# Linear ReLU attention: four engine programs jump to a fresh instruction block at the start, and wait for the last store at the end

## The chip, the core and the metric

The kernel runs on one core of a Trainium2 chip. A core has five engines, each with a program of its own: TensorE (PE in the tables; its weight loads are PEld), VectorE (DVE), ScalarE (ACT), GpSimd (POOL) and SyncE (SP). They meet through semaphores. Data moves between the large memory (HBM) and the on-chip memory (SBUF) by DMA, issued here by SP, ACT and POOL and carried out by 16 DMA engines. The metric is the device time of one launch in microseconds (us), lower is better.

## The reference

Q, K and V have shape (8, 12, 512, 64), that is 96 heads of 512 rows, in 32-bit floats. Each head is independent:

```python
Q_feat = np.maximum(0, Q)
K_feat = np.maximum(0, K)
KV = np.einsum('bhkd,bhkv->bhdv', K_feat, V)
K_sum = np.sum(K_feat, axis=2)
numerator = np.einsum('bhqd,bhdv->bhqv', Q_feat, KV)
denominator = np.einsum('bhqd,bhd->bhq', Q_feat, K_sum)
return numerator / (denominator[:, :, :, None] + 1e-10)
```

## The kernel before, in words

The work is cut into NO = 12 blocks of 8 heads. A block of Q, of K or of V is 1 MB in HBM, 128 partitions of 8 KB each, and a block of the output is 1 MB as well, so 48 such transfers are all the traffic. Most loads turn the numbers into bf16 on their way, so 512 KB arrive in SBUF.

The program of each engine is written out by hand in the order of the source; no scheduler moves anything.

- SP issues the load of K of block 0 (line 94), and at the end the stores of the last two blocks (`store`, line 117, called from line 134). Then it waits for the semaphores of all 12 stores (line 318) and clears the semaphores (line 321).
- ACT issues the load of V of block 0 (line 95). Its first compute instruction waits for ID to be 4 (line 207), which says that the masks are there. For each block it then moves results from PSUM to SBUF.
- POOL issues Q of block 0 (line 96), makes the identity matrix (lines 119 and 121), and then issues the loads of blocks 1 to 11 in the order K, V, Q (`load`, line 109). The ring of input buffers holds RING = 6 blocks, so from block 7 on a load waits until its buffer has been read. In between it issues the stores of blocks 0 to 9 (line 117), each as soon as `norm` has written that block.
- DVE clears buffers and builds masks (lines 276 to 295), adds the last step to ID, and then for each block prepares K and V (`prep`, lines 237 and 241), copies Q (`stage`, line 247), and divides (`denominators`, lines 265 to 273, and `norm`, line 259).
- PE waits for ID to be 4, then runs a loop of 12 turns (line 189). A turn (`turn`) transposes Q (line 158), multiplies K with V (line 167), transposes the previous block's results back (`back`, line 148), and computes the denominators (line 176) and numerators (line 184) of its own. After the loop, `back(0)` and `back(1)` do the transposes of the last block. The loop's head is put at the start of a 256-instruction block of PE's program by the loop's `head_slot` argument; the builder emits an alignment and a jump for that.

The output buffer ring has NOUT = 9 blocks, so `norm` of blocks 9, 10 and 11 waits until the store of the block nine before has ended. Each store has a semaphore of its own, `stored[o]`, and every DMA adds 16 to its semaphore, one for each DMA engine that has finished its part.

The times further down rest on how instructions get to an engine: the trace shows DMA packets of kind "instruction" on two queues of their own, q8 and q14.

Of the kernel before, what the change touches and what calls it, by code (L numbers as in the profile page):

```python
# [5 lines left out]
def kernel(  # L6
# [18 lines left out]
    NO = B * H // 8  # L25
    assert NO * 8 == B * H and R == 16
    RING = 6
    NOUT = 9
    RUNS = (1,) * 11
    HEAD = 4  # L30

# [4 lines left out]
    PE, PL, VE, AC, SP = nc.tensor, nc.gpsimd, nc.vector, nc.scalar, nc.sync  # L36
# [6 lines left out]
    def sb(name, shape, dt):  # L43
        return nc.alloc_sbuf_tensor(name, shape, dt)[:]
# [3 lines left out]
    def sems(*names):  # L48
        new = [nc.alloc_semaphore(n) for n in names]
        handles.extend(new)  # L50
        return new
# [8 lines left out]
    q_all = sb("q_all", [P, RING + 1, U * P], bf16)  # L60
    o_sb = [sb(f"o_sb{i}", [P, RQ, D], fp32) for i in range(NOUT)]
    k8, v8 = o_sb[0], o_sb[1]
# [18 lines left out]
    ID, STG, PR0, PR1, DEN, NRM0, NRM1, DV = sems(  # L81
        "id", "stg", "pr0", "pr1", "den", "nrm0", "nrm1", "dv")
# [1 line left out]
    CQ0, CQ1, CK0, CK1, CB0, CB1, CD, CO0, CO1 = sems(  # L84
        "cq0", "cq1", "ck0", "ck1", "cb0", "cb1", "cd", "co0", "co1")
    landed = {}
    stored = sems(*[f"st{o}" for o in range(NO)])

    def land(name):
        landed[name], = sems(name)  # L90
        return landed[name]


    SP.dma_start(out=k8.rearrange("p r d -> p (r d)"), in_=Kr[0]).then_inc(land("k0"), 16)
    AC.dma_start(out=v8.rearrange("p r d -> p (r d)"), in_=Vr[0]).then_inc(land("v0"), 16)
    PL.dma_start(out=q_all[:, RING], in_=Qr[0], single_packet=True).then_inc(land("q0"), 16)  # L96
    run_of = {0: 0}

# [15 lines left out]
    def store(eng, o):  # L114
        eng.wait_ge(NRM1, o + 2)
        kw = {"single_packet": True} if eng is PL else {}
        eng.dma_start(out=Or[o], in_=o_sb[(o + 2) % NOUT].rearrange("p r d -> p (r d)"), **kw).then_inc(stored[o], 16)  # L117

# [4 lines left out]
    o, done = 1, 0  # L123
    for n in RUNS:
        while done < o + n - 1 - RING - HEAD + 1:
# [4 lines left out]
    assert o == NO  # L130
    for i in range(done, NO - 2):
        store(PL, i)
    for i in range(NO - 2, NO):
        store(SP, i)

# [10 lines left out]
    def back(j):  # L146
        for v in range(8):
            t = PE.transpose(ps_o[j][:, P * v:P * v + P], ot[:, 8 * j + v].rearrange("p h c -> p (h c)"), ident32)  # L148
        t.then_inc((CB0, CB1)[j], 1)
# [35 lines left out]
                              start=True, stop=True, skip_group_check=True)  # L185
            t.then_inc((CO0, CO1)[j], 1)

    PE.wait_ge(ID, 4)
    with nc.Fori(1, NO + 1, engines=bass.OrderedEngineSet([PE.engine]), head_slot={PE.engine: 0}) as i:
        turn(i)  # L190
    PE.wait_ge(OT, NO + 1)
    back(0)
    back(1)


    def v_rows(o, g):
# [7 lines left out]
    def v_scalar(o):  # L204
        arrived(AC, "v", o)
        if o == 0:
            AC.wait_ge(ID, 4)
        AC.activation(vo[0][:, :, 1, 2:D + 2], v_rows(o, 0), Act.Copy, scale=mask_v[:, 1:2]).then_inc(VC, 1)  # L208

    v_scalar(0)  # L210
    for o in range(NO):
        for j in range(2):
            AC.wait_ge((CQ0, CQ1)[j], o + 1)
            AC.activation(qt_sb[:, j * (U // 2):(j + 1) * (U // 2)],  # L214
                          ps_q[j].bitcast(bf16).rearrange("p (u f) -> p u f", u=U // 2), Act.Relu)
        AC.wait_ge(CK1, o + 1)
        for s in range(2):
            for c in range(2):
                t = AC.copy(  # L219
                    kvd[64 * c:64 * c + 64, s::2, c * D1:c * D1 + D1].rearrange("p (g t) d -> p g t d", t=2),  # L220
                    ps_kv[64 * s:64 * s + 64, :, 0:2 * (D + 2)].rearrange(
                        "p g (t d) -> p g t d", t=2)[:, :, :, c:c + D1])
        t.then_inc(KVD, 1)
        if o + 1 < NO:
            v_scalar(o + 1)
        for j in range(2):
            AC.wait_ge((CO0, CO1)[j], o + 1)
            t = AC.copy(ot[:, :, 4 * j:4 * j + 4],  # L228
                        ps_o[j].rearrange("p (h u c) -> p u h c", h=4, u=U))
        t.then_inc(OT, 1)  # L230


    def prep(o, g):

        arrived(VE, "k", o)
        for s in range(2):
            VE.tensor_scalar(kf[g][:, :, s, :], k_rows(o, g), scalar1=0.0,  # L237
                             scalar2=mask_k[:, s:s + 1], op0=Alu.max, op1=Alu.mult)
        arrived(VE, "v", o)
        for t in range(1 + g):  # L240
            x = VE.tensor_scalar(vo[g][:, :, t, 2:D + 2], v_rows(o, g), scalar1=mask_v[:, t:t + 1],  # L241
                                 scalar2=None, op0=Alu.mult)
        x.then_inc((PR0, PR1)[g], 1)
# [5 lines left out]
    def norm(o):  # L249
        dst = o_sb[(o + 2) % NOUT]  # L250
        if o >= NOUT:
            VE.wait_ge(stored[o - NOUT], 16)
        VE.wait_ge(DV, 2 * o + 2 + DV0)
        if o == NOUT - 1:
            VE.wait_ge(VC, 1)
        for j in range(2):
            rs = slice(R * j, R * j + R)
            VE.wait_ge((CB0, CB1)[j], o + 2)
            VE.tensor_tensor(dst[:, rs], ps_o[j].rearrange("p (r d) -> p r d", d=D),  # L259
                             rec[o % 2][:, rs].unsqueeze(2).to_broadcast([P, R, D]),  # L260
                             op=Alu.mult).then_inc((NRM0, NRM1)[j], 1)
# [42 lines left out]
    for o in range(NO):  # L304
# [7 lines left out]
        if o + 1 < NO:  # L312
            prep(o + 1, 1)
    norm(NO - 1)


    for s in stored:
        SP.wait_ge(s, 16)
    used = sorted(s.num for s in handles)
    assert used == list(range(used[0], used[-1] + 1))  # L320
    SP.sem_clear(range(used[0], used[-1] + 1))
# [28 lines left out]
```

## Time and profile before

| | |
|---|---|
| median of three runs | 124.9 us (124.57 to 125.02) |
| the profiled execution's own time | 124.66 us |
| its span, first to last instruction | 123.4 us |
| busy: DVE, PE, ACT, POOL | 89.3, 87.4, 79.4, 27.5 us |
| HBM read and written | 37.75 and 12.58 MB |
| loads issued by POOL, issue to landing | 33.1 to 36.7 us |
| the last two stores, issued by SP, issue to landing | 8.4 us |

The page has a row for each engine with its busy share in 40 slices of the span, one for the DMA engines in the same slices, a table of the DMA queues, the chain of work that ended last, and the costliest groups of instructions. A group's row gives its line, engine and operation, the tiles, the count, the busy time, the mean duration, and how long the engine stood idle just before it and for what. A table by stage gives for each stretch of the span the busy time of PE, PEld, DVE, ACT and POOL with the number of instructions, the granted TensorE clock, the share of the DMA engines in use and the GB/s that they moved.

### The profile page before, as it was taken

To read this page: it belongs to the slowest core of one execution; us is meant where nothing else is said; L and a number is where in the kernel's file an instruction comes from. 1 tells how busy PE (TensorE), PEld (TensorE's weight loads), DVE (VectorE), ACT (ScalarE), POOL (GpSimd) and SP (SyncE) were. 2 spreads that over 40 slices of the span, in tenths; PEclk is the share of its full clock that TensorE was granted. 3 is DMA by queue.
4 is the path that set the end of the run, shared out by engine and by line. 5 is a ranking of instruction groups with operands and counts; after the bars stand their busy time and mean duration, and the time that the engine had idled before them with its cause. 6 is when DMAs were issued, how large, how long until landed. Compare 5 with 4: busy or idle time off the path is not lost.

```text
span 123.4 us, 3380 instructions
## 1 busy us (share of the span) xinstructions
PE 87.4 (71%) x1456; PEld 75.9 (62%) x1456; DVE 89.3 (72%) x178; ACT 79.4 (64%) x109; POOL 27.5 (22%) x50
## 2 busy tenths in 40 slices
PE   0000099998998979799897998979449939977400
PEld 0000099986886868688686877958429928947200
DVE  3737906599989899998989989897395497091600
ACT  0043063999988888898888889888539649542000
POOL 3999500050240804309101001010010001000000
PEclk9999999999999999999999999999985995996775
DMA  3999999999999999999999999999999999999994
GB/s 43 369 344 217 213 213 213 213 215 213 214 213 213 213 215 213 214 214 217 214 213 214 213 214 221 371 217 214 375 222 214 343 425 428 425 422 433 420 425 170
DMA packets 6918, 32.57 MB, mean 264 GB/s; under 512 B 768, under 2 KB 768, under 8 KB 5120
## 3 DMA queue, kind: packets, MB, share of 16 engines
q0 software_dynamic: 6336, 28.31, 92.2%
q1 hardware_dynamic: 432, 3.15, 6.6%
q10 hardware_dynamic: 144, 1.05, 2.2%
q8 instruction: 2, 0.03, 0.1%
q14 instruction: 4, 0.03, 0.1%
HBM read 37.75 MB, written 12.58 MB: 408 GB/s over the span
## 4 chain that ended last, share of the span: by engine, by line
DMA 34%; issue 27%; POOL 18%; PE 8%; DVE 5%; ACT 1%; POOLq 0%; DVEq 0%
DMA q_all<-in_Q_dram 34%; POOL k_all L109 6%; POOL q_all L109 5%; POOL v_all L109 5%; DVE o_sb L259 5%; PE ps_o L148 4%; PE ps_kv L167 2%; PE ps_q L158 1%; PE ps_o L184 1%; POOL out_dram L117 1%; ACT ot L228 1%; POOL q_all L96 1%; POOL ident L121 0%; POOL ident L119 0%; POOLq L107 0%
## 5 line engine op out<-in xcount | busy, mean ns | idle before, releaser
L259 DVE TENSOR_TENSOR o_sb<-ps_o,rec 128x1024 f32<-128x1024 f32 x24 | 28.3, 1219 | 7.0 <-PE ps_o L148 6.7
L228 ACT COPY ot<-ps_o 128x1024 f32<-128x1024 f32 x24 | 24.2, 1013 | 10.3 <-PE ps_o L184 9.2
L167 PE MATMUL ps_kv<-vo,kf 64*128 64x132 bf16 x768 | 28.6, 230 | 0.7
L148 PE MATMUL ps_o<-ident,ot 128*128 128x128 f32 x208 | 27.1, 286 | 1.1 <-ACT ot L228 1.1
L167 PEld LDWEIGHTS ps_kv<-vo,kf 64*128 64x128 bf16 x768 | 24.8, 100 | 3.8 <-DVE vo L241 2.3
L214 ACT ACTIVATE qt_sb<-ps_q 128x1024 bf16<-128x1024 bf16 x24 | 23.4, 1030 | 5.1 <-PE ps_q L158 5.1
L158 PE MATMUL ps_q<-ident,q_sb 128*128 128x128 bf16 x192 | 15.3, 243 | 15.4 <-DVE q_sb L247 15.4
L148 PEld LDWEIGHTS ps_o<-ident,ot 128*128 128x128 f32 x208 | 23.8, 146 | 2.7 <-ACT ot L228 1.4
L158 PEld LDWEIGHTS ps_q<-ident,q_sb 128*128 128x128 bf16 x192 | 13.2, 110 | 16.7 <-DVE q_sb L247 15.4
L219 ACT CAST kvd<-ps_kv 64x260 bf16<-64x260 f32 x48 | 18.0, 375 | 7.8 <-PE ps_kv L167 7.4
L184 PE MATMUL ps_o<-qt_sb,kvd 128*128 128x256 bf16 x96 | 15.0, 282 | 10.8 <-DVE o_sb L259 9.8
L237 DVE TENSOR_SCALAR kf<-k_all,mask_k 128x1024 bf16<-128x1024 bf16 x44 | 18.3, 459 | 5.6 <-PE ps_kv L167 5.4
L184 PEld LDWEIGHTS ps_o<-qt_sb,kvd 128*128 128x128 bf16 x96 | 7.7, 100 | 15.6 <-DVE o_sb L259 15.0
L241 DVE TENSOR_SCALAR vo<-v_all,mask_v 128x1024 bf16<-128x1024 bf16 x33 | 15.0, 483 | 0.9 <-DMA v_all<-in_V_dram 0.9
L109 POOL DMA_DIRECT2D k_all<-in_K_dram x11 | 8.4, 763 | 32.1 <-DVE vo L241 32.0
L117 POOL DMA_DIRECT2D out_dram<-o_sb x10 | 5.3, 533 | 40.7 <-DVE o_sb L259 40.7
L208 ACT ACTIVATE vo<-v_all,mask_v 128x1024 bf16<-128x1024 bf16 x11 | 12.7, 1155 | 0.3
L247 DVE COPY q_sb<-q_all 128x2048 bf16<-128x2048 bf16 x12 | 8.3, 694 | 5.7 <-DMA q_all<-in_Q_dram 5.7
L109 POOL DMA_DIRECT2D q_all<-in_Q_dram x11 | 8.9, 811 | 0.0
L109 POOL DMA_DIRECT2D v_all<-in_V_dram x11 | 7.6, 687 | 0.0
L176 PE MATMUL ps_q<-kvd,qt_sb 128*128 128x16 bf16 x192 | 6.9, 180 | 0.0
L176 PEld LDWEIGHTS ps_q<-kvd,qt_sb 128*128 128x128 bf16 x192 | 6.7, 96 | 0.2
(24 smaller groups left out, 27.8 us busy)
## 6 DMA issues: line engine op xcount, KB each, us to landing
out_dram<-o_sb POOLq DMA_DIRECT2D x10, 1024.0 KB, 39.8
q_all<-in_Q_dram POOLq DMA_DIRECT2D x12, 512.0 KB, 36.7
k_all<-in_K_dram POOLq DMA_DIRECT2D x11, 512.0 KB, 33.1
v_all<-in_V_dram POOLq DMA_DIRECT2D x11, 512.0 KB, 34.8
out_dram<-o_sb SPq DMA_DIRECT2D x2, 1024.0 KB, 8.4
o_sb<-in_K_dram SPq DMA_DIRECT2D x1, 1024.0 KB, 8.5
o_sb<-in_V_dram ACTq DMA_DIRECT2D x1, 1024.0 KB, 8.8
```

The source lines that it names most:

```text
L109: PL.dma_start(out=t[:, to:to + n], in_=X[o:o + n].rearrange("n p f -> p n f"), single_packet=True).then_inc(land(f"{c}{o}"), 16)
L148: t = PE.transpose(ps_o[j][:, P * v:P * v + P], ot[:, 8 * j + v].rearrange("p h c -> p (h c)"), ident32)
L158: t = PE.transpose(dst[:, u], q_sb[:, j * (U // 2) + u], ident)
L167: t = PE.matmul(ps_kv[:, half, 0:2 * (D + 2)].rearrange("p (t d) -> p t d", t=2), kf[g][rows, r].rearrange("p s d -> p (s d)"), vo[g][rows ...
L176: t = PE.matmul(ps_den[:, u], qt_sb[:, u], kvd[:, :, 0:2 * D1:2 * D1 - 1], start=True, stop=True, skip_group_check=True)
L184: t = PE.matmul(ps[:, h], kvd[:, 4 * j + h, 1:2 * D + 1], q[:, :, 4 * j + h, :], start=True, stop=True, skip_group_check=True)
L214: AC.activation(qt_sb[:, j * (U // 2):(j + 1) * (U // 2)], ps_q[j].bitcast(bf16).rearrange("p (u f) -> p u f", u=U // 2), Act.Relu)
L219: t = AC.copy(kvd[64 * c:64 * c + 64, s::2, c * D1:c * D1 + D1].rearrange("p (g t) d -> p g t d", t=2), ps_kv[64 * s:64 * s + 64, :, 0:2 * ...
L228: t = AC.copy(ot[:, :, 4 * j:4 * j + 4], ps_o[j].rearrange("p (h u c) -> p u h c", h=4, u=U))
L237: VE.tensor_scalar(kf[g][:, :, s, :], k_rows(o, g), scalar1=0.0, scalar2=mask_k[:, s:s + 1], op0=Alu.max, op1=Alu.mult)
L241: x = VE.tensor_scalar(vo[g][:, :, t, 2:D + 2], v_rows(o, g), scalar1=mask_v[:, t:t + 1], scalar2=None, op0=Alu.mult)
L259: VE.tensor_tensor(dst[:, rs], ps_o[j].rearrange("p (r d) -> p r d", d=D), rec[o % 2][:, rs].unsqueeze(2).to_broadcast([P, R, D]), op=Alu. ...
```

## The change

There are four edits. They compute nothing and move no data.

1. `at_line(eng)` emits an alignment: the next instruction of that engine's program stands at a multiple of FETCH = 128 instructions, and the engine gets there by a jump (no fill of empty instructions is allowed, `max_nops=0`). It is put into POOL's, ACT's and DVE's programs. On ACT it stands behind the issue of V of block 0; on POOL ahead of the issue of Q of block 0; on DVE ahead of its first instruction. SP gets none.
2. PE no longer waits for ID ahead of its loop, so that it jumps to the loop's block at once, and waits for its first tile there.
3. The stores' semaphores are merged: the stores of blocks 0, 1 and 2, which `norm` waits for, keep their own; those of blocks 3 to 9 share ALL, those of blocks 10 and 11 share LAST.
4. `hold(eng)` is put at the end of POOL's, PE's, ACT's and DVE's programs: it waits until ALL and LAST are complete, and then adds 1 to FIN. SP waits for FIN to be 4 in place of its twelve semaphores. On POOL the hold comes after its last store, on PE after `back(1)`.

```diff
+    FETCH = 128
...
-    stored = sems(*[f"st{o}" for o in range(NO)])
+
+    ALL, LAST, FIN = sems("all", "last", "fin")
+    stored = [sems(f"st{o}")[0] if o + NOUT < NO else ALL if o < NO - 2 else LAST for o in range(NO)]
...
+    def at_line(eng):
+
+        eng.addr_align(FETCH, offset=0, max_nops=0)
+
+    def hold(eng):
+
+        eng.wait_ge(ALL, 16 * (NOUT - 2))
+        eng.wait_ge(LAST, 32)
+        eng.sem_inc(FIN, 1)
+
...
     AC.dma_start(out=v8.rearrange("p r d -> p (r d)"), in_=Vr[0]).then_inc(land("v0"), 16)
+    for eng in (PL, AC, VE):
+        at_line(eng)
     PL.dma_start(out=q_all[:, RING], in_=Qr[0], single_packet=True).then_inc(land("q0"), 16)
...
         store(PL, i)
+    hold(PL)
     for i in range(NO - 2, NO):
         store(SP, i)
...
-    PE.wait_ge(ID, 4)
     with nc.Fori(1, NO + 1, engines=bass.OrderedEngineSet([PE.engine]), head_slot={PE.engine: 0}) as i:
         turn(i)
     PE.wait_ge(OT, NO + 1)
     back(0)
     back(1)
+    hold(PE)
...
         t.then_inc(OT, 1)
+
+    hold(AC)
...
     norm(NO - 1)
-
-
-    for s in stored:
-        SP.wait_ge(s, 16)
+    hold(VE)
+
+
+    SP.wait_ge(FIN, 4)
```

## The prediction

> **What bounds the kernel now.** I read the page's slices first, then its queues, then stages of the span, then single DMA windows, and last the trace's record of every DMA packet (queue, start, duration, size).
>
> ```profile
> span 123.4 us, 3380 instructions
> DMA  3999999999999999999999999999999999999994
> q8 instruction: 2, 0.03, 0.1%
> q14 instruction: 4, 0.03, 0.1%
> HBM read 37.75 MB, written 12.58 MB: 408 GB/s over the span
> ```
>
> The DMA row is full from the second slice to the last but one while no compute engine is above 72% busy. The packet records say the same: from 2.75 us on all 16 DMA engines work without a gap, an 8 KB packet every 0.307 us each. So the end is the start of the DMA stream, plus each engine's own packets, plus whatever else is put on that engine. Two small queues are something else: six packets of instructions, 16 KB on q8, 8 KB on q14. Windows of the DMA view place them:
>
> ```profile
> q8 instruction: 1, 0.02, 2.9%
> ...
> q14 instruction: 1, 0.01, 1.3%
> ...
> q14 instruction: 1, 0.01, 1.0%
> ...
> q8 instruction: 1, 0.02, 3.0%
> ```
>
> These come from the windows 11 to 13, 32 to 33.5 (97 to 98.5 and 105 to 106.5 show the same row), 49 to 51 and 114 to 116 us. By the packet records: q8 at 11.495 us (935 ns) and 114.339 (965 ns); q14 at 32.745 and 49.661 (322 ns), 97.455 and 105.547 (309 ns).
>
> Whose are they? DVE has begun 58 instructions by 29.0 us and 186 by 93.7, exactly 128 apart, and its two fetches would then lie 3.75 us later each, at 32.745 and 97.455. The same 3.75 us before the others: 7.74 us, when PE's jump into its loop (started 7.347, 309 ns) ends; 45.9, ACT's 46th instruction; 101.8, POOL's last; 110.59, PE just after its loop.
>
> ```profile
> L189 PEldq COMPARE_BRANCH  x13: 76/208/309, 7.3 to 110.3; - x13
> 2.70:121.20 118.50, 87.39 (x1456) 75.89 (x1456) 88.47 (x175) 79.39 (x109) 26.54 (x45) 0.95 1.04 273
> 121.20:121.60 0.40, 0.00 (x0) 0.00 (x0) 0.00 (x0) 0.00 (x0) 0.00 (x0) 0.50 0.31 123
> 121.60:122.20 0.60, 0.00 (x0) 0.00 (x0) 0.00 (x0) 0.00 (x0) 0.00 (x0) 0.50 0.23 96
> 122.40:122.70 0.30, 0.00 (x0) 0.00 (x0) 0.00 (x0) 0.00 (x0) 0.00 (x0) 0.50 0.07 27
> ```
>
> The first row is the loop's branch; the last leaves the loop at 110.279 + 0.076 = 110.355. Then stages of the span: the DMA share (last but one column) falls from full to 0.31, 0.23, 0.07. 0.23 of 16 is 3.7 engines: four are still working when twelve have ended. Laying each engine's packets end to end, twelve end at 121.20 to 121.59 us (middle 121.35), four at 122.22, 122.34, 122.69 and 122.715. The late ones are those that carried the fetches of 105.5 (POOL), 97.5 (DVE), 11.5 (PE) and 114.3 us (PE). A fetch costs its engine its packet and a longer packet behind it: among reads 0.3 to 0.4 us for 8 KB (322 and 0.04), 1.1 for 16 KB; among stores 0.3 (+0.35 at 97.5, +0.09 at 105.5) and for 16 KB 0.965 + 0.355 = 1.3. The lag is never made up. The last store's last landing is at 123.129 us, SP's final wait passes, and the clear ends the span:
>
> ```profile
> L318 SPq EVENT_SEMAPHORE  x6: 17/28/28, 117.0 to 123.1; - x6
> L321 SPq EVENT_SEMAPHORE_RANGE_CLEAR  x1: 145/145/145, 123.2 to 123.2; - x1
> ```
>
> The profiled execution took 124.66 us, 1.30 outside its span; the median of the three runs, 124.9, is 0.24 above it.
>
> **The change part by part.**
>
> **Jumps on POOL, ACT, DVE.** Each is one jump into a new block. The nearest row is PE's own: branch and next instruction 7.347 to 7.782, 0.44 us. Bounds: 0.2 (a taken branch inside the loop, 208 ns) and a full fetch of 3.75 us if the target is not there. I take 0.44, the same kind of jump. Six 8 KB fetches stand before the span (10.4 to 7.6 us before it), so targets should be there.
> - POOL: its jump stands ahead of the first Q load (issued 1.93 us, first packets 6.31), the identity memset, and all 33 loads behind. K and V of block 0, issued by SP and ACT at 1.40 before any jump, keep the DMA engines busy alone until about 8.1 (2.41 + 1.1 for the first packet, 15 more at 0.307). Slack 8.1 - 6.31 = 1.8 us against 0.44: nothing.
> - DVE: memsets and masks end at 7.2, K of block 0 lands at 9.94; the row "DVE kf L237 <- DMA o_sb<-in_K_dram" waits 2.8. Nothing. ACT waits for the masks (7.3), then a 1.28 us table load, and V lands at 10.15: 7.74 + 1.28 = 9.0. Nothing.
>
> **PE's wait for the masks removed.** PE enters its loop near 1.7 instead of 7.7 us and waits there for its first tile (ready 15.4, so the wait is only moved). Nothing on PE's work.
>
> **Fetches moved.** POOL's goes from 105.5, ACT's from 49.7, DVE's first from 32.7, PE's first from 11.5, to 1.7 us plus 1.0 (SP's K issue at 1.40 to its packets at 2.41, idle engines) to 3.75: start 2.7 to 5.5 us. That is mostly behind the first data, so each still costs its engine: 0.3 for 8 KB, 0.6 (two packets' time) to 1.1 for PE's 16 KB. DVE's remaining program, 210 - 6 = 204 instructions, fits no single block of 128; it crosses once at about its 134th instruction (64 to 66 us), a fetch near 69 among reads, 0.35. Engine ends from these: POOL's and ACT's 121.35 + 0.3 = 121.65, DVE's two 121.7, PE's first 122.0 to 122.7.
>
> **PE's second fetch stays.** PE's loop is 240 weight loads and matmuls, a move, a semaphore wait, an add and a branch: 244 of the 256 that 16 KB hold. Behind it come 32 more (`back(0)`, `back(1)`), so 12 instructions after leaving the loop PE steps into the next block, and 110.355 plus 12 issues of some 20 ns is 110.6, the 110.59 from above. The new `hold(PE)` comes after those 32. Neither the jump nor the hold moves this crossing, and the fetch at 114.3 still costs 1.3 on an engine that carries no other: 122.715, as before. That is why I count the other gains at nothing: this engine was already the last by 0.02 us.
>
> **The end.** SP's six waits (all but the last two long met) become one on FIN. After the last landing each of four engines passes a wait and adds to FIN, then SP clears. Before, landing to clear was 123.129 to 123.211, 0.08. New: an engine's wait (17 to 51 ns in the opening barrier's records), a hand-over (0.04, POOL's release at 0.621 to SP's next at 0.663), about 0.13: +0.05. Nothing is queued behind the holds; POOL's last store is ahead of its hold. What the engines do after the program now starts together instead of having been waiting: bounds 0 and 1.3 (all time outside the span once more); nearest, one opening barrier, 0.33. SP itself leaves last, as before, so I take 0 and keep 0.33 for the range.
>
> **Sum.** DMA start 0, last engine 122.715 - 0.0, end +0.05: 124.66 + 0.05 = 124.71 for such an execution, 0.24 more for the median: **124.95 us**.
>
> The Trainium skill, "Runtime: NRT & Kernel Launch", section "Instruction fetch mechanics", calls the price of crossing a block "one DMA tail-bump, mostly hidden", with blocks of 16 KiB. The trace shows 8 KB for all but PE, and the crossing hidden for the engine, but not for the DMA engine that carries it (0.3 to 1.3 us); by the page nothing could be won at all, which here gives the same sum.
>
> **The rivals.**
>
> *Faster: the last PE fetch goes too.* If it were caused by what follows PE's program, and not by the 12th instruction after the loop, the hold would put it behind the end. For: POOL's fetch came just at its end too. Against: the 3.75 us fit the crossing to 0.05 us; DVE's and ACT's ends brought none. Then the last engine is the one with PE's early fetch, 122.0 to 122.7: gain 0 to 0.7; if that packet comes before 2.4 us and is hidden, 121.7 and a gain of 1.0. I give 124.9 + 0.05 - 0.8 = 124.15, up to 123.9.
>
> *Slower: a jump's target has to be fetched.* Then POOL stands still 1.0 + 0.3 us (idle engines) to 3.75. The decisive point is 1.8 us: beyond it the DMA engines run dry between block 0's K and V and the first Q. 3.75 + 0.3 - 1.8 = 2.2 at worst, 127.1; 126.0 in the middle. Against: the six fetches before the span and PE's 0.44 us jump.
>
> The same page says, in the same section, that a taken branch to a target outside the two-page window stalls for a DMA fetch. No row here shows such a stall, and PE's jump to its next block did not.
>
> *Slower: the ends.* Holding four engines back lengthens what follows the last instruction by more than 0.6 us: 125.6 to 126.2. The 1.30 us outside the span allow it; the 0.33 us barrier speaks against it.
>
> *Fetches meet on one DMA engine.* Here all six lay on different ones. A PE and an 8 KB fetch on one: +0.3, 125.25.
>
> **How the numbers follow.** 0.5% (0.62 us) is about what a measurement can tell from no change. No change by the above, collisions included: 0.57. Faster rival 0.2, jump stall 0.13, ends 0.10. The first alone spans 124.4 to 125.4 (the 0.33 and 0.3 above, the scatter of runs of 0.2 below). To leave out no more than 2 in 10 the range reaches half into the rivals: 124.1 to 125.8.
>
> **What would show it.** Right: q8 still shows one packet near 114; q14 none after about 70 us; the share in the stage after the twelve engines end falls to one or two engines (0.06 to 0.12) instead of 0.23, yet the clear still starts at about 123.25; jumps on POOL, ACT, DVE of 0.2 to 0.5 us; first Q packets near 6.7. Wrong: no q8 packet after 100 us and an end before 122.6; POOL's first load after 4 us and a gap in the DMA row near 8 to 10; or a time outside the span well over 1.3 us.

## The result and the profile after

The changed kernel takes 125.35 us (median of 17 runs, 124.84 to 126.42), the kernel before 124.82 us (17 runs): a ratio of 1.0054, 95% interval 1.0034 to 1.0074. It is slower, clear of the noise; whether by more than the half per cent that I had set as the bound of "no change" the interval leaves open. 124.95 us was forecast, and the time lies inside the range of 124.1 to 125.8.

Each run lists its time and its span, so the time outside the span is their difference. Its median is 1.74 us after the change (17 runs, 1.67 to 1.82) and 1.33 us before (the 35 runs of the kernel before that were made with the first experiments, 1.26 to 1.46): +0.41. The median span is 123.6 against 123.5 us: +0.1, small beside the scatter of the spans before, 123.0 to 124.4. Together that is nearly the 0.53 between the medians. The profiled execution is one of the slower ones, 125.88 us: 1.79 outside a span of 124.09.

The page of the changed kernel, first lines, DMA row and instruction queues:

```profile
span 124.1 us, 3381 instructions
DMA  2999999999999999999999999999999999999994
q14 instruction: 4, 0.03, 0.1%
q8 instruction: 2, 0.03, 0.1%
```

There are still six instruction packets, but elsewhere. The DMA view of the windows 2 to 3, 4 to 7 (two rows), 68 to 70 and 114 to 116 us:

```profile
q14 instruction: 1, 0.01, 10.6%
...
q8 instruction: 1, 0.02, 2.2%
q14 instruction: 2, 0.02, 1.4%
...
q14 instruction: 1, 0.01, 1.0%
...
q8 instruction: 1, 0.02, 3.0%
```

The packet records give 2.43, 4.52, 5.12 (PE's), 6.30, 69.03 and 114.89 us (PE's second). Now the start on POOL, first after the change, then before:

```profile
5.05 0.67 POOL L111 DMA_DIRECT2D q_all<-in_Q_dram  x1 [4.60 <-issue]
5.72 0.22 POOL L134 MEMSET ident<- 128x128 bf16 x1
```

```profile
1.93 0.67 POOL L96 DMA_DIRECT2D q_all<-in_Q_dram  x1 [1.48 <-POOLq L16]
```

The first Q load issues 3.1 us later, and its first packets come at 7.97 us, 1.7 later than the 6.31 of before. What that does to the DMA engines is in the stages (DMA share and GB/s are the last two columns), after and then before:

```profile
2.70:7.50 4.80, 0.00 (x0) 0.00 (x0) 3.53 (x19) 0.00 (x0) 2.04 (x5) 1.00 0.89 357
7.50:9.25 1.75, 0.00 (x0) 0.00 (x0) 0.28 (x2) 1.28 (x1) 1.75 (x4) 1.00 0.96 260
...
121.20:121.60 0.40, 0.00 (x0) 0.00 (x0) 0.00 (x0) 0.00 (x0) 0.00 (x0) 0.50 0.97 410
121.60:122.20 0.60, 0.00 (x0) 0.00 (x0) 0.00 (x0) 0.00 (x0) 0.00 (x0) 0.50 0.72 300
122.40:122.70 0.30, 0.00 (x0) 0.00 (x0) 0.00 (x0) 0.00 (x0) 0.00 (x0) 0.50 0.26 109
122.70:123.40 0.70, 0.00 (x0) 0.00 (x0) 0.00 (x0) 0.00 (x0) 0.00 (x0) 0.50 0.09 35
```

```profile
2.70:7.50 4.80, 0.00 (x0) 0.00 (x0) 3.61 (x19) 0.20 (x1) 4.40 (x10) 1.00 0.89 332
7.50:9.25 1.75, 0.00 (x0) 0.00 (x0) 0.00 (x0) 1.08 (x1) 1.75 (x5) 1.00 1.01 346
```

From 7.5 to 9.25 us the rate falls from 346 to 260 GB/s: on several DMA engines K and V of block 0 run out before Q comes. Part of the fall is the type alone: a Q packet is listed with the 4 KB that it writes as bf16 and takes 0.32 us, a packet of K with 8 KB and 0.31. But the share drops too, by the packet records to 12 of 16 engines at work near 8.5 us, and some of the first Q packets are listed with 1.36 and 1.40 us instead of 0.32; I take it that they wait for their first data. By 11 us 347 data packets have ended, 388 before, and 41 packets of 0.32 us on 16 engines are 0.8 us. The median landing of the first Q block moves from 11.07 to 11.94 us, that of the 28th transfer from 72.61 to 73.38, the last landing from 123.13 to 123.89. So in this execution the whole stream is 0.8 us late, and at 121.6 to 122.2, where 0.23 of the DMA engines were at work before, 0.72 are. The profiled execution is one of the 4 of 17 whose span is 124.1 or longer; in the median the spans differ by the 0.1 from above.

The end, the four holds and SP's clear:

```profile
L104 ACTq EVENT_SEMAPHORE  x1: 1823/1823/1823, 122.1 to 122.1; - x1
L104 POOLq EVENT_SEMAPHORE  x1: 1823/1823/1823, 122.1 to 122.1; - x1
L104 DVEq EVENT_SEMAPHORE  x1: 1825/1825/1825, 122.1 to 122.1; - x1
L104 PEldq EVENT_SEMAPHORE  x1: 1823/1823/1823, 122.1 to 122.1; - x1
...
L339 SPq EVENT_SEMAPHORE_RANGE_CLEAR  x1: 135/135/135, 124.0 to 124.0; - x1
```

The rows are each hold's second wait, the one for LAST: it begins when ALL is full, at 122.1, and takes 1.82 us. From the last landing (123.891) to the clear (123.954) it is 0.063 us, before it was 0.082: inside the span the new ending costs nothing. What it costs comes behind the last instruction.

### The profile page after: what moved, and what is told of

Read it like the earlier page. It is cut to its first block, busy times and chain, and to the rows that moved or that the text cites. A ratio compares the mean times of both kernels' runs of the same rounds, so it can differ in the third digit from the quotient of the medians.

```text
span 124.1 us, 3381 instructions
## 1 busy us (share of the span) xinstructions
PE 86.6 (70%) x1456; PEld 75.1 (60%) x1456; DVE 89.0 (72%) x178; ACT 79.4 (64%) x109; POOL 27.9 (23%) x50
## 4 chain that ended last, share of the span: by engine, by line
DMA 34%; issue 28%; POOL 18%; PE 8%; DVE 5%; ACT 1%; POOLq 0%; DVEq 0%
DMA q_all<-in_Q_dram 34%; POOL k_all L124 6%; POOL q_all L124 6%; POOL v_all L124 5%; DVE o_sb L277 5%; PE ps_o L164 4%; PE ps_kv L183 2%; PE ps_q L174 1%; PE ps_o L200 1%; POOL out_dram L132 1%; ACT ot L244 1%; POOL q_all L111 1%; POOL ident L136 0%; POOL ident L134 0%; POOLq L122 0%
## 5 line engine op out<-in xcount | busy, mean ns | idle before, releaser
L183 PE MATMUL ps_kv<-vo,kf 64*128 64x132 bf16 x768 | 27.4, 224 | 0.7
L183 PEld LDWEIGHTS ps_kv<-vo,kf 64*128 64x128 bf16 x768 | 23.6, 97 | 3.9 <-DVE vo L259 2.3
L200 PE MATMUL ps_o<-qt_sb,kvd 128*128 128x256 bf16 x96 | 15.5, 289 | 11.3 <-DVE o_sb L277 10.7
L124 POOL DMA_DIRECT2D k_all<-in_K_dram x11 | 7.3, 661 | 29.5 <-DVE vo L259 29.3
L124 POOL DMA_DIRECT2D q_all<-in_Q_dram x11 | 8.3, 758 | 0.0
```

What stands on the lines that cost most here:

```text
L124: PL.dma_start(out=t[:, to:to + n], in_=X[o:o + n].rearrange("n p f -> p n f"), single_packet=True).then_inc(land(f"{c}{o}"), 16)
L183: t = PE.matmul(ps_kv[:, half, 0:2 * (D + 2)].rearrange("p (t d) -> p t d", t=2), kf[g][rows, r].rearrange("p s d -> p (s d)"), vo[g][rows ...
L200: t = PE.matmul(ps[:, h], kvd[:, 4 * j + h, 1:2 * D + 1], q[:, :, 4 * j + h, :], start=True, stop=True, skip_group_check=True)
```

## The experiments

**Which half of the change costs?** Two theories. E: the holds cost, outside the span, because what each engine does behind its program now begins only after the last store. J: the jumps cost, in the span and behind it, because the ends of the programs lie elsewhere in their blocks. First each half alone.

Holds without jumps (this diff and the next are against the changed kernel):

```diff
-    for eng in (PL, AC, VE):
-        at_line(eng)
...
+    PE.wait_ge(ID, 4)
     with nc.Fori(1, NO + 1, ...
```

> The kernel before with edits 3 and 4 alone: merged store semaphores, holds on four engines, FIN; no jumps, and PE waits for the masks again. Theory E (the holds cost, because what each engine does behind the program now starts together): time outside the span 1.75 us as after the change (1.30 before), span 123.3 to 123.5 as before, so 125.25 to 125.3 against 124.8. Theory J (the jumps cost, in the span and behind it, because the engines' ends lie elsewhere in their blocks): outside 1.30, time 124.8 as before.

Measured: 125.12 us (12 runs) against 124.9 (35 runs, shared by the first four kernels). Time outside the span 1.75 in the median, span 123.35 against 123.5. E names the outside right, to the hundredth; the span came out 0.15 shorter than it was before, so the total is 0.15 below what E expected, and the ratio of 1.0015 (0.9993 to 1.0036) alone would not tell it from no change. What tells it is the time outside the span, 1.65 to 1.83 in 12 runs against 1.26 to 1.46 before.

Jumps without holds, and the stores' semaphores as before:

```diff
-    def hold(eng):
...
-    hold(PL)
...
-    SP.wait_ge(FIN, 4)
+    for s in stored:
+        SP.wait_ge(s, 16)
```

> The kernel before with edits 1 and 2 alone: jumps on POOL, ACT and DVE, PE enters its loop at once; twelve store semaphores and SP's waits as before, no holds. Theory E: outside 1.30, span 123.1 to 124.6 as after, middle 123.55, time 124.85. Theory J: outside 1.75, time 125.3. Both: POOL's first load issues near 5.05 us, not 1.93.

Measured: 125.02 us, outside 1.31, spans 123.3 to 124.6 with a median of 123.65; POOL's first load at 5.148. E holds, J's second half falls: the jumps change nothing behind the program. What they may cost is in the span: 0.15 us in the median, which the ratio of 1.0017 (0.9991 to 1.0044) does not tell from nothing, and 3 of 12 spans of 124.1 or longer, against 3 of 35 before.

**Which engine's hold?** The hold-only kernel again, with the hold on one engine at a time; for PE, for instance (against the hold-only kernel):

```diff
-    hold(PL)
...
-    hold(AC)
...
-    hold(VE)
...
-    SP.wait_ge(FIN, 4)
+    SP.wait_ge(FIN, 1)
```

> The hold-only kernel with the hold on POOL alone; SP waits for FIN to be 1. If one engine's way out of the program is the slow one, one of the four single holds shows the time outside the span of 1.75 us and the others 1.30 to 1.35. If it is that all come at once, each of the four shows less than 1.75, between 1.30 and 1.6.

> The same with the hold on PE alone: outside 1.75 if PE's way out is the slow one, 1.30 to 1.35 if not; in between if it is that all come at once.

> The same with the hold on ACT alone: outside 1.75 if ACT's way out is the slow one, 1.30 to 1.35 if not; in between if it is that all come at once.

> The same with the hold on DVE alone: outside 1.75 if DVE's way out is the slow one, 1.30 to 1.35 if not; in between if it is that all come at once.

One execution each, its time and its span to the nanosecond (the second row, the kernel before run beside the four, has its span to 0.1 us only):

| held besides SP | time, us | span, us | outside, us |
|---|---|---|---|
| none (before) | 124.66 | 123.356 | 1.30 |
| none (before, beside the four) | 124.59 | 123.2 | 1.39 |
| ACT | 124.95 | 123.619 | 1.33 |
| DVE | 125.21 | 123.808 | 1.40 |
| PE | 125.20 | 123.670 | 1.53 |
| POOL | 125.15 | 123.450 | 1.70 |
| all four (hold only) | 125.16 | 123.475 | 1.69 |

It is one engine's way out, POOL's: held alone it costs as much as all four. ACT and DVE lie inside the scatter of the kernel before, 1.26 to 1.46, so nothing is shown of them. PE's 1.53 lies just above it; 12 runs each of two kernels further down that hold PE alone give 1.45 and 1.48 in the median, 0.12 to 0.15 above the 1.33 of before. I had expected all but one to be at 1.30 to 1.35. The merged semaphores cost nothing to be seen: ACT's kernel has them too. All four held cost no more than POOL: the ways out add up to no more than the slowest. My reading, which no trace shows because they end with SP's clear, is that they run beside each other, and that before the change all of them but SP's ran while the last stores were still moving.

**What does POOL's stall cost?** The changed kernel without POOL's jump:

```diff
-    for eng in (PL, AC, VE):
+    for eng in (AC, VE):
```

> The changed kernel without POOL's jump. If POOL's stall of 3.7 us is what makes the DMA engines run dry near 8 to 9 us in the profiled execution after, POOL's first load is back at 1.93 us, the dip is gone, and the last landing comes 0.4 to 0.8 earlier than the 123.89 there; the scatter of the spans (123.1 to 124.6) shrinks. POOL's own block then ends near its last store again, but its hold waits there: no fetch at 105. Time outside 1.75 by theory E: 125.0 to 125.2.

Measured: 125.36 us, span 123.65 (123.1 to 124.0), outside 1.70. In its profile POOL's first load is back at 1.923, the dip at 7.5 to 9.25 is gone, the first Q block's median landing is at 11.19 instead of 11.94, and the last landing is at 123.46, 0.43 earlier: as expected. No span is over 124.0 us, where 124.6 was reached. The median did not move, 125.36 and not 125.0 to 125.2: a miss. And a packet on q14 is there at 105.64, where I had expected none: POOL reaches its next block before it stands in its hold.

This kernel and the one with the holds alone have the same ending and differ in the jumps of ACT and DVE and in PE's early start. Their spans are 123.65 (123.1 to 124.0) and 123.35 us (123.0 to 123.5), 12 runs each, and the times 125.36 and 125.12: 0.24 more, with a 95% interval of 0.09 to 0.44 from drawing the runs anew. So beside the holds this part does cost time, and POOL's jump adds nothing to the median. PE's early start, which brings its first fetch forward, is the suspect, because a kernel below with ACT's and DVE's jumps and without PE's early start has its median span at 123.65 us against 123.6 of before. It was not run alone.

POOL's jump alone, in the kernel before:

```diff
+    at_line(PL)
     PL.dma_start(out=q_all[:, RING], in_=Qr[0], single_packet=True).then_inc(land("q0"), 16)
```

> The kernel before with POOL's jump alone. Only one early fetch on q14 is POOL's, so its time can be laid beside POOL's first load. If the jump's target has to be fetched: a packet of 8 KB that ends just before POOL's first load (5.05 after the change), and possibly a second one behind it. If the target was there: a packet behind the jump that POOL does not wait for, first load near 2 us. With the stall and the slack of 1.8 us the span grows by 0.5 to 1.9; outside 1.30. Time 124.8 (no stall) to 126.5.

Measured: 125.01 us, ratio 1.0007 (0.9977 to 1.0038), spans 122.9 to 124.9, outside 1.33. The first load issues at 4.994; the one early packet on q14 runs from 2.47 to 4.07, 0.92 us before it. The first Q packets come at 8.10, just as K and V run out: the share from 7.5 to 9.25 us stays at 1.04, and the first Q block's median landing is only 0.09 later than before, though two of its packets take 1.79 and 1.87 us and two DMA engines land it 1.4 us late. In the two profiles with the other engines' fetches among K and V, those of the changed kernel and of the jumps alone, it did not fit; that the fetches are why is argued only. The issue came 3.1 us later but the packets only 1.8, so the delay of an issue is not that of its data.

Where the early jump of POOL shows is in the tail. Spans of 124.1 us or longer came in 12 of 41 runs of the three kernels that have it (4 of 17, 3 of 12, 5 of 12), in none of the 24 of the two without it (holds alone, no POOL jump), and in 3 of the 35 and, beside the later experiments, 5 of the 29 of before. So the jump is not their only cause, and the counts are a hint, no more.

**Is it the block that POOL waits for?** The same jump with the identity's two instructions ahead of the first Q load:

```diff
+    at_line(PL)
-    PL.dma_start(out=q_all[:, RING], in_=Qr[0], single_packet=True).then_inc(land("q0"), 16)
     ...
     PL.memset(ident, 0.0).then_inc(ID, 1)
     ...
                      pattern=[[-1, P]], channel_multiplier=1).then_inc(ID, 1)
+    PL.dma_start(out=q_all[:, RING], in_=Qr[0], single_packet=True).then_inc(land("q0"), 16)
```

> POOL's jump alone, at the start, but with the identity memset and select (lines 134 and 136 of the changed kernel) ahead of the first Q load, so that the first instruction behind the jump is no DMA. If POOL stands still because the block that it jumps to has to be fetched, the memset starts only near 5 us, after the end of the 8 KB packet (near 4.1), and everything behind it is as late. If only the first DMA issue is held up (by whatever the jump does to it), the memset starts near 1.9 us and the Q load near 5 us. DVE waits for the identity, so in the first case its mask chain is 3.5 us late as well.

Its timeline on POOL (start, duration, and in brackets the idle time before):

```profile
1.82 0.20 POOL L123 MEMSET ident<- 128x128 bf16 x1 [1.38 <-POOLq L16]
2.27 0.28 POOL L125 TENSOR_SCALAR_AFFINE_SELECT ident<-ident 128x128 bf16<-128x128 bf16 x1 [0.24 <-POOL ident L123]
4.59 0.68 POOL L127 DMA_DIRECT2D q_all<-in_Q_dram  x1 [2.04 <-issue]
```

The memset behind the jump starts at 1.82 us, 0.47 behind the jump's start at 1.353. POOL's instruction packet starts only at 2.43. So the target block is there, and the jump costs POOL what it costs PE. Only the DMA issue is held up, to 4.59, for 2.04 us in which nothing that the profile shows is waited for. I had expected 1.9 and 5.0 for this case. It may wait for that packet: in the two runs in which it is the only early one on q14, the jump alone and this one, it ends at 4.07 and 3.47 us, and the issue follows 0.92 and 1.12 us behind. That it does is not shown. The run took 125.14 us, the kernel before beside it 125.27, one execution each.

Does a later jump do it too? Jumps on ACT and DVE at the start, on POOL ahead of block 7's load, no holds:

```diff
+    for eng in (AC, VE):
+        at_line(eng)
...
     for n in RUNS:
+        if o == RING + 1:
+            at_line(PL)
```

> The kernel before with jumps on ACT and DVE at the start and on POOL only ahead of the load of block 7, near 14 us, where POOL has nothing to do until 25.9 us; no holds, PE waits for the masks as before. If POOL's stall comes from the jump itself and not from its place, a packet of 8 KB on q14 starts some 3.75 us behind the jump, and a second one only if POOL also asks for the block after it; the stall is hidden, POOL's load of block 7 issues at 25.9 as before. No q14 packet after 75 us. Theory that PE's second fetch sets the end: time as before, 124.8 to 124.95, outside 1.30. Rival, that fewer late fetches shorten the end: 124.3 or less.

POOL's sequencer reaches the jump at 10.72 us, ahead of the last loads that it has queued. The timeline:

```profile
10.30 0.62 POOL L115 DMA_DIRECT2D v_all<-in_V_dram  x1
10.82 0.86 POOL L115 DMA_DIRECT2D q_all<-in_Q_dram  x1
...
25.94 0.78 POOL L115 DMA_DIRECT2D k_all<-in_K_dram  x1 [12.28 <-DVE vo L249]
```

The loads that go on at 10.82 us stand ahead of the jump in POOL's program. One packet on q14 follows at 14.30, 3.6 us behind the jump, and none after 75 us; block 7's load, the first issue behind the jump, goes at 25.94 as before, when DVE has freed its buffer. So the late jump costs nothing, but not because no stall is possible: an issue held up by 3 us behind it would have been hidden in the wait of 12 us for the buffer. Whether the jump as such holds up the next issue, or only a jump ahead of the first one, stays open, and so does what the issue waits for; a jump directly behind the first Q load would have told more and wasn't tried.

The time is 125.01 us against 124.93 (29 runs of before), ratio 0.9996 (0.9970 to 1.0023), outside 1.30, span 123.65 against 123.6: with the late 8 KB fetches of POOL and DVE gone and nothing paid for it, the time is the same. The rival's 124.3 or less does not come.

**Does PE's second fetch set the end?** With 4 of 16 transposes behind the loop, PE stays in its loop's block (PE alone is held):

```diff
-    back(0)
-    back(1)
+    back(0, 2)
+    back(1, 2)
     hold(PE)
```

> The kernel with the hold on PE alone (outside 1.53), with 4 of the 16 transposes behind PE's loop: PE then stays in its loop's block. Twelve transposes of the last block's results are left out, so most of that block's output is not computed. Theory: no q8 packet near 114, and one late DMA engine fewer; the engine with PE's first fetch is then the last, 0.02 us earlier by the profile before, so the span stays at 123.2 to 123.6. Rival, that PE's second fetch alone makes the end late: span 122.9 or less (the next two engines end 0.38 and 0.49 earlier).

> The two together: 4 of 16 transposes behind the loop and the hold on PE, jumps on ACT and DVE at the start and on POOL near 14 us. The same twelve transposes are left out. Only PE's first fetch (16 KB near 11.5 us, lag 1.1 to 1.3) and 8 KB fetches among reads (0.3 to 0.4) are left: one DMA engine alone is late in the last store. Theory: span 123.1 to 123.4 all the same, since that one engine sets it; outside 1.53. Rival, that the number of late engines counts and not the last one: span 122.5 or less.

The first: no packet on q8 near 114, so it is the crossing that fetches, as read from the trace of before. Span 123.35 (123.1 to 123.6) against 123.6 (123.2 to 124.8): inside the expected 123.2 to 123.6; the rival's 122.9 or less does not come. The second: span 123.3 (123.2 to 123.5). Again inside, and 122.5 is far. In both the last store is issued 1.8 to 2.3 us earlier (114.89 and 114.33 us in the profiles, 116.67 before), because twelve transposes are left out; even so the end does not come earlier by more than 0.25 to 0.3. But my picture of one late engine alone was wrong. Its stages at the end:

```profile
121.60:122.20 0.60, 0.00 (x0) 0.00 (x0) 0.00 (x0) 0.00 (x0) 0.00 (x0) 0.50 0.20 82
122.40:122.70 0.30, 0.00 (x0) 0.00 (x0) 0.00 (x0) 0.00 (x0) 0.00 (x0) 0.50 0.13 55
```

0.20 of 16 is three engines, and the last store lands at 122.81, 123.26 and 123.32 on three of them. The lag of a DMA engine is the landing of its part of a transfer less the median landing of the 16 parts. Among the loads one engine lags by 1.2 us from 13.8 us on (PE's 16 KB fetch), one by 0.74 from the first load on (an early 8 KB fetch, dearer than the 0.3 to 0.4 of a later one), and the second one's lag rises to 1.2 at 70 us, when DVE's fetch of 69.5 us has come on the same engine. Two fetches did meet there. Times: 124.84 and 124.80 us, ratios 0.9987 (0.9961 to 1.0014) and 0.9985 (0.9960 to 1.0010), with 0.15 us of PE's hold in both; neither is told from the kernel before.

No version here is told to beat the kernel before. PE's 16 KB fetch on entering its loop's block alone keeps one DMA engine 1.1 to 1.3 us late, and starting it at 5.1 instead of 11.5 us made it dearer: in the changed kernel without POOL's jump one engine lags by 2.0 us on K of block 0 and by 1.7 on every load behind it, against 1.2 before.

## Why the prediction was right, and where it was not

The time is inside the range, 0.40 us above the forecast and half way to the upper bound, and the ratio's interval, 1.0034 to 1.0074, holds the bound between "within 0.5%" and "slower". The sum forecast +0.05 us; measured were +0.53. That the range held is no luck, since the nearest row for the end, 0.33, was kept in it; but the sum itself took 0 there, and of the signs named for being wrong two came, the second in part: the time outside the span, 1.74 us, and POOL's first load after 4 us, with a dip to 12 of 16 DMA engines near 8.5, though the row of slices shows no gap. The sign for being right that only one or two DMA engines would still be at work at the end did not come: the last store lands late on four of them, by 0.61, 0.68, 1.06 and 1.27 us.

- **The end: the term that failed.** The prediction had "bounds 0 and 1.3 (all time outside the span once more); nearest, one opening barrier, 0.33. SP itself leaves last, as before, so I take 0 and keep 0.33 for the range." Measured: +0.41 in the medians, 1.70 with POOL alone held. The mechanism was named and the nearest row was near; the reason for taking 0 was wrong. That SP leaves last says nothing of how long the others take to leave, and POOL takes 0.3 to 0.4 us longer than SP. The inside part, +0.05, was -0.02.
- **PE's second fetch stays, and the other gains count for nothing**: right. The fetch is at 114.89, and it goes when the crossing goes. Even without it, the engine with PE's first fetch keeps the end where it was, to 0.25 us at most.
- **Fetches moved**: four came at 2.4 to 6.3 us (2.7 to 5.5 expected), DVE's at 69.03 (69). Their price was set too low: PE's was taken at 0.6 to 1.1 us and cost up to 2.0 (without POOL's jump; in the changed kernel one engine is 2.2 us late on K of block 0 and 1.3 from Q on), one early 8 KB fetch 0.7 instead of 0.3.
- **Jumps**: DVE's took 0.6 us (1.423 to 2.030, expected 0.44), and nothing waited for it; ACT's lies under the masks. For POOL "nothing" was wrong in the execution profiled after: its DMA issue was held up 3.1 us against a slack of 1.8, and the stream came 0.8 us late. The point at which K and V run out, 8.1 us, was read well. The slack was not, because it took a delay of the issue for the same delay of the packets, and these came only 1.7 to 1.8 us later; that is why so long a stall cost so little, and as far as the sum goes it was luck. In the medians the jumps and PE's early start cost 0.1 to 0.15 us against the kernel before, which is not told from nothing, and 0.24 against the holds alone, which is; leaving POOL's out moved the median by 0.01.
- **The rival of the jump** had the right place and, with 3.1 us, a stall inside its 1.3 to 3.75; its price for the whole, 126.0 to 127.1 us, did not come, and its mechanism was not the one seen: with the memset ahead the block was there and a compute instruction ran at once. The rule that the Trainium skill gives in "Runtime: NRT & Kernel Launch", section "Instruction fetch mechanics", a stall for a branch out of the two-page window, is not seen here: PE's jump took 0.44 us, DVE's 0.6, POOL's 0.47 to its first compute instruction. Whether these targets lie outside that window no run shows.
- **The faster rival** fell with PE's second fetch, which came before the hold, as the 3.75 us had said.

## What to carry to other kernels

An engine that has finished should not be held until the last store without need: here POOL's cost 0.3 to 0.4 us behind the last store, and nothing to be seen where POOL was not held. A fetch of instructions costs the one DMA engine that carries it, and where all DMA engines are full, as here, this shows at the end as a few late landings of the last store; moving it to the start of the same full stream saved nothing. Of several late engines only the last one counts, so read the next one's time before you count a gain.

## What the runs showed of the hardware

- Time outside the span by the engine that is held besides SP: POOL 1.70 us (1.65 to 1.83 in 12 runs with all four held); PE 1.53, and 1.45 and 1.48 in the medians of 12 runs; ACT 1.33 and DVE 1.40 are not told from none, 1.26 to 1.46.
- A jump ahead of POOL's first DMA issue held that issue up to 4.6 to 5.15 us (1.93 without it), while a compute instruction put directly behind such a jump started after 0.47 us. A jump at 10.7 us cost nothing, with no issue due behind it for 15 us.
- A DMA engine's lag stays: without POOL's jump one engine's 1.7 us from the first Q on is still 1.6 at 98 us. In the changed kernel, where the stream ran dry for a moment, four engines were 0.7 to 2.2 us late on K of block 0 and only one, by 1.3 us, on the first Q. That is no rule: with the jumps alone three were 0.6 to 2.1 us late on K, and three 0.8 to 1.4 us on Q.
